# Layer 1's modulation products moved from the middle of a SwiGLU to its edges, in a two-layer diffusion block

## The chip, the cores and the metric

The kernel runs on one core of one Trainium2 chip. The metric is device time in microseconds (us) of one execution of the program. Every time below comes from the runs of the kernel before or from one profiled execution of it.

## The reference, cut to what matters

A block of two layers works on 512 latent tokens and 256 context tokens of width 1024. In each layer the stream is normalised, scaled and shifted by six modulation vectors that come from a conditioning vector `c` (for context tokens from `c_ctx`), goes through a mixer, and then the same again through a SwiGLU of width 2816. Layer 0's mixer is a long convolution beside a gating MLP. Layer 1's is a recurrent block, which puts out latent tokens only.

```python
def swiglu(h, w_in, w_out):
    z = h @ w_in
    return (jax.nn.silu(z[..., :D_FF]) * z[..., D_FF:]) @ w_out

silu_c = jax.nn.silu(c)
silu_cc = jax.nn.silu(c_ctx)
for l in range(DEPTH):
    mod_x = (silu_c @ w_ada[l] + b_ada[l]).reshape(-1, 1, N_MOD, D_MODEL)
    hx = modulate(rmsnorm(x, norm_mix_g[l]), mod_x[:, :, 0], mod_x[:, :, 1])
    ...
    x = x + mod_x[:, :, 2] * mix_x
    hx = modulate(rmsnorm(x, norm_ffn_g[l]), mod_x[:, :, 3], mod_x[:, :, 4])
    x = x + mod_x[:, :, 5] * swiglu(hx, w_ffn_in[l], w_ffn_out[l])
```

The change concerns `silu_c @ w_ada[l]` and `silu_cc @ w_ada[l]` for `l` = 1. `w_ada[1]` has 1024 x 6144 floats, 24 MB. Vectors 0 and 1 are needed when layer 1 begins, vector 2 when the recurrent block's result is added to the stream, vectors 3 to 5 in layer 1's SwiGLU.

## The kernel before, in words

Matrices are multiplied on PE in a split form: each operand becomes a high and a low part (`hh`/`hl`, `whi`/`wlo`), and three products (high by high, low by high, high by low) go into one accumulator. Weights come by DMA from SP's queue into `raw` tiles (lines 231 and 1420), and are split into `whi` and `wlo` by ACT, DVE and POOL (lines 248 and 249). PSUM has two `mm` tiles of two banks and four `sm` tiles of one bank (lines 208 to 212).

**Modulation products.** `Ada(l, r)` makes modulation vectors 2r and 2r+1 of layer l, for `c` and `c_ctx`, as one set, in eight steps k. `load(k)` brings a piece of `w_ada` of 128 x 2048 floats, 1 MB, from SP's queue (line 329). `mm(k)` makes four matmuls of 128 rows by 32 columns, each over 512 elements, side by side in one `sm` tile that is held until the eighth step (line 338; the trace has two records for each of these matmuls). After the eighth, ACT copies the tile to `adas` (line 342), PE transposes it in four pieces, and DVE adds `b_ada` into `mod[l][r]`. For layer 1 the loads go through one buffer of 8 KB a partition, of which `adas` is a use too, so a load waits for the matmuls of the step ahead of it.

**Where they stand before.** `fill` is a list of 24 steps, `Ada(1, 0)`, `Ada(1, 1)` and `Ada(1, 2)` in a row. `ffn` is layer 0's SwiGLU on 768 tokens. It takes 22 pairs of columns in parts of four (`PARTS`, line 59): for each pair the two input products and the gating, and after each part the part's share of the output product, with weights `wfo`. `post(j)` pops one step after pair j, or two.

**The order of the work.** Programs are written as Python loops, and a scheduler orders each engine's instructions by dependencies and by the priorities of the places that are written down. Each engine then runs its instructions in that order and waits where the next one isn't ready. SP issues all these DMAs in one order too.

**What surrounds the new places.** `Norm.start` (line 423) begins a layer half: it applies the norm to the first block of tokens for k = 0 to 7, with the first products of each k behind it, then to the second block; in the middle of the first loop it makes the second block's statistics (`stats`, matmuls with `ones`, line 394) and broadcasts them (`bc`, line 402, the transposes of `ny`). `out_units` (line 1079) is a generator over the tiles of an output projection, and `out_proj` runs all of it. In the recurrent stage `mix` interleaves the head products of chunk j+1 with a chain of units: input products, gate products, and output-projection units `w_out`. Between chunks, tiles change partitions by the DMAs `hx<-xl` and `th<-tg` on SP. The last units, `w_out(9, 11)`, come after the loop over 11 chunks.

## Time and profile before

| | |
|---|---|
| median of 3 runs | 1840.28 us (1839.06 to 1844.47) |
| profiled execution, own time | 1839.97 us |
| its span, first to last instruction | 1838.2 us |
| mean granted TensorE clock | 0.959 of full speed |
| PE busy | 1695.2 us, 92% of the span |
| DVE busy | 1271.3 us, 69% |
| ACT busy | 726.6 us, 40% |
| POOL busy | 622.0 us, 34% |
| DMA on SP's and the other hardware queues | 204.67 MB |

In the span, layer 0's SwiGLU begins at about 475 us; its pairs end at about 1028. The last of its output products lasts to about 1051, layer 1's norm and first products to 1087. The recurrent stage runs from there to about 1420, its last out-projection to 1433, and layer 1's SwiGLU and the final norm take the rest.

Busy time of an engine is the sum of its instructions, and of PE it overlaps, since matmuls are pipelined. "Idle before" in a timeline is the time that the engine waited ahead of the instruction, with what ended the wait. A granted clock of 1.00 is 2.4 GHz, 0.50 is 1.2 GHz; a stretch's figure is a mean of the two.

### The profile page before, as it was taken

To read this page: it belongs to the slowest core of one execution; us is meant where nothing else is said; L and a number is where in the kernel's file an instruction comes from. 1 tells how busy PE (TensorE), PEld (TensorE's weight loads), DVE (VectorE), ACT (ScalarE), POOL (GpSimd) and SP (SyncE) were. 2 spreads that over 40 slices of the span, in tenths; PEclk is the share of its full clock that TensorE was granted. 3 is DMA by queue.
4 is the path that set the end of the run, shared out by engine and by line. 5 is a ranking of instruction groups with operands and counts; after the bars stand their busy time and mean duration, and the time that the engine had idled before them with its cause. 6 is when DMAs were issued, how large, how long until landed. Compare 5 with 4: busy or idle time off the path is not lost. (4 is left out here: it accounts for less than half of the span.)

```text
span 1838.2 us, 23815 instructions
## 1 busy us (share of the span) xinstructions
PE 1695.2 (92%) x8968; PEld 1436.0 (78%) x8968; DVE 1271.3 (69%) x1963; ACT 726.6 (40%) x1144; POOL 622.0 (34%) x518
## 2 busy tenths in 40 slices
PE   5999999889989999999999897988986799999996
PEld 2576888679878989898899776777775778888885
DVE  7875766684887878887888876789888733333225
ACT  3543332222443333433343436665754332322212
POOL 4333132442455555564645412343353200000002
PEclk8999999999999999999999998988998899999998
DMA  8746232634223342224321224444443132222321
GB/s 288 232 139 233 89 120 72 245 111 150 78 106 115 116 147 105 69 92 132 143 71 63 74 80 116 121 124 121 113 119 104 47 122 96 92 92 81 91 81 46
DMA packets 78396, 213.00 MB, mean 116 GB/s; under 512 B 7609, under 2 KB 33353, under 8 KB 74185
## 3 DMA queue, kind: packets, MB, share of 16 engines
q1 hardware_dynamic: 75913, 204.67, 34.3%
q0 software_dynamic: 1792, 6.29, 1.0%
q8 instruction: 70, 1.15, 0.3%
q10 hardware_dynamic: 576, 0.52, 0.1%
q14 instruction: 45, 0.37, 0.1%
HBM read 178.30 MB, written 11.53 MB: 103 GB/s over the span
## 5 line engine op out<-in xcount | busy, mean ns | idle before, releaser
L249 DVE TENSOR_TENSOR wlo<-raw,whi 128x512 fp32r<-128x512 f32 (+2 forms) x300 | 310.0, 1050 | 264.3 <-ACT whi L248 257.0
L248 ACT CAST whi<-raw 128x1024 fp32r<-128x1024 f32 (+2 forms) x228 | 193.5, 858 | 430.4 <-PE mm L264 179.5
L387 POOL TENSOR_TENSOR ssum<-ssum,sq 128x256 f32<-128x256 f32 (+2 forms) x37 | 37.4, 1015 | 448.0 <-ACT sq L385 417.0
L249 POOL TENSOR_TENSOR wlo<-raw,whi 128x1024 fp32r<-128x1024 f32 (+1 forms) x31 | 77.7, 2506 | 129.4 <-DVE whi L248 42.6
L1110 PE MATMUL sm<-yh,whi 128*128 128x256 f32 (+1 forms) x304 | 97.5, 327 | 21.3 <-DVE x L1073 12.9
L287 PE MATMUL sm<-hh,whi 128*128 128x512 f32 (+1 forms) x248 | 94.9, 383 | 10.3 <-ACT whi L248 5.7
L1110 PE MATMUL sm<-yl,whi 128*128 128x256 f32 (+1 forms) x304 | 96.8, 318 | 2.5 <-DVE yl L257 2.5
L1110 PE MATMUL sm<-yh,wlo 128*128 128x256 f32 (+1 forms) x304 | 96.3, 317 | 0.0
L287 PE MATMUL sm<-hh,wlo 128*128 128x256 f32 (+1 forms) x248 | 92.8, 380 | 3.5 <-POOL wlo L249 2.8
L287 PE MATMUL sm<-hl,whi 128*128 128x512 f32 (+1 forms) x248 | 93.5, 377 | 0.0
L338 PE MATMUL sm<-ada,sct 128*32 128x512 f32 x384 | 77.6, 630 | 4.7 <-DMA ada<-in_w_ada_dram 3.0
L248 DVE CAST whi<-raw 128x512 fp32r<-128x512 f32 (+2 forms) x103 | 70.9, 688 | 15.9 <-PE sm L1285 12.1
L1110 PEld LDWEIGHTS sm<-yh,whi 128*128 128x128 f32 x304 | 60.9, 202 | 26.2 <-DVE x L1073 14.1
L264 PE MATMUL mm<-hl,whi 128*128 128x512 f32 (+1 forms) x256 | 69.4, 346 | 0.0
L264 PE MATMUL mm<-hh,wlo 128*128 128x512 f32 (+1 forms) x256 | 69.1, 347 | 0.0
L264 PE MATMUL mm<-hh,whi 128*128 128x512 f32 (+1 forms) x256 | 68.1, 345 | 0.0
L287 PEld LDWEIGHTS sm<-hh,whi 128*128 128x128 f32 x248 | 50.5, 203 | 21.0 <-ACT whi L248 8.1
L1651 ACT ACTIVATE tg<-mm,hba 88x768 f32<-88x768 f32 x64 | 55.3, 892 | 23.4 <-PE mm L264 13.3
L1110 PEld LDWEIGHTS sm<-yl,whi 128*128 128x128 f32 x304 | 61.7, 203 | 2.7 <-DVE yl L257 2.7
L1110 PEld LDWEIGHTS sm<-yh,wlo 128*128 128x128 f32 x304 | 61.4, 202 | 0.1
L287 PEld LDWEIGHTS sm<-hh,wlo 128*128 128x128 f32 x248 | 50.4, 204 | 12.6 <-POOL wlo L249 3.2
L1327 POOL TENSOR_TENSOR u<-u,u 128x384 f32<-128x384 f32 x40 | 51.4, 1285 | 25.5 <-ACT u L1326 25.5
(942 smaller groups left out, 5307.9 us busy)
## 6 DMA issues: line engine op xcount, KB each, us to landing
raw<-in_wfi_dram SPq DMA_DIRECT2D x88, 512.0 KB
ada<-in_w_ada_dram SPq DMA_DIRECT2D x32, 1024.0 KB
raw<-in_wfo_dram SPq DMA_DIRECT2D x38, 512.0 KB
ada<-in_w_ada_dram SPq DMA_DIRECT2D x24, 512.0 KB
raw<-in_wio_dram SPq DMA_DIRECT2D x22, 512.0 KB
raw<-in_wie_dram SPq DMA_DIRECT2D x20, 512.0 KB
th<-tg SPq DMA_DIRECT2D x12, 528.0 KB
kk<-kdx SPq DMA_DIRECT2D x16, 384.0 KB
```

Of the source, the lines that this page charges most:

```text
L248: (h_.tensor_copy if h_ is not act else act.copy)(hi, src)
L249: l_.tensor_sub(lo, src, f(hi))
L264: pe.matmul(o, w, xx, start=(k == 0 and pi == 0), stop=(k == n - 1 and pi == 2))
L287: pe.matmul(self.outs[b], w[:, k * P:(k + 1) * P], x, start=(n == 0 and pi == 0), stop=(n == self.nk - 1 and pi == 2))
L338: pe.matmul(self.ps[32 * q:32 * q + 32, :], sct[:, 2 * k:2 * k + 32], self.w[k, q], start=(k == 0), stop=(k == KD - 1))
L387: (dve if late else pool).tensor_add(self.s[b], self.s[b], q)
L1110: pe.matmul(pa, w[:, c], x[k][:, t0 - off:t1 - off], start=(i == 0 and pi == 0), stop=(i == n - 1 and pi == 2))
L1327: pool.tensor_add(v, v, u)
L1651: act.activation(h3(t[:, mi, :]), m[0:RDH, :, 0:384], AF.Tanh, bias=hba[:, b:b + 1], scale=0.5)
```

## The change

The steps no longer lie in a list that the SwiGLU's pairs pop. `Ada.units()` is a generator of eight units; each makes one step's products and then issues the next step's load. Set 0 is handed to `Norm.start` of layer 0's SwiGLU, which takes one unit at every second k of both loops. Set 1 (`late`) gives four units in layer 0's last output projection and four in layer 1's `Norm.start`. Set 2 (`last_mods`) goes in the recurrent loop, two units in chunk 8, two in chunk 9 and four in chunk 10. The buffer's pool `adaB` is opened later, in space that the convolution stage frees, and closed later. `g4`, which needs set 1, is computed after layer 1's start.

```diff
@@ -1,3 +1,4 @@
+import itertools
 import math
 
 import numpy as np
@@ -358,6 +359,15 @@
                 return go
             return [step(k) for k in range(KD)]
 
+        def units(self):
+
+            self.load(0)
+            for k in range(KD):
+                self.mm(k)
+                if k + 1 < KD:
+                    self.load(k + 1)
+                yield
+
     def ab(l, which):
         g = pc(f"mix_g{l}" if which == "mix" else f"ffn_g{l}")
         sc = mod[l][0][:, :, 8:16] if which == "mix" else mod[l][2][:, :, 0:8]
@@ -420,22 +430,26 @@
                 dve.scalar_tensor_tensor(hl[:, c], ta[:, c], self.sh[:, v, k:k + 1], f(hh[:, c]),
                                          op0=ALU.add, op1=ALU.subtract)
 
-        def start(self, jobs, order=range(KD), then=None):
+        def start(self, jobs, order=range(KD), then=None, fill=iter(())):
 
             for i, k in enumerate(order):
                 self.apply(0, k)
                 for j in jobs:
                     j.mm(0, k)
+                if i % 2:
+                    next(fill, None)
                 if i == 3:
                     self.stats(1)
                 if i == 6:
                     self.bc(1)
-            for k in order:
+            for i, k in enumerate(order):
                 self.apply(1, k)
                 if then:
                     then(k)
                 for j in jobs:
                     j.mm(1, k)
+                if i % 2:
+                    next(fill, None)
 
     def htiles(pl):
         hh = [pl.tile([P, T], F32R, tag=f"hh{k}", name=nm("hh")) for k in range(KD)]
@@ -1055,8 +1069,6 @@
     _, c2 = op("c2")
     _, xp = op("x")
     cm_xc, xc = op("xc")
-    cm_ada, ada["p"] = op("adaB")
-    ada.update(b=1, w=2048)
     cm_nt, ntp = op("ntB")
     cm_g, gp = op("g0")
     xt = []
@@ -1141,8 +1153,10 @@
     out_proj(lambda m: A["woe"][m], [4, 5, 6, 7, 0, 1, 2, 3], yh, yl, 0, mod[0][1][:, :, 0:8], FB0, nrm, 6)
     cl(cm_za)
     cl(cm_zb)
-
-    def ffn(l, blks, nrm, ntp, gp, hf, fill, done, nblks):
+    cm_ada, ada["p"] = op("adaB", "right")
+    ada.update(b=1, w=2048)
+
+    def ffn(l, blks, nrm, ntp, gp, hf, fill, late, done, nblks):
 
         off, h = blks[0][0], blks[0][1] - blks[0][0]
         n = 2 * h
@@ -1203,17 +1217,12 @@
         def halves(m):
             return [m[:, 0, n0], m[:, 1, n0]]
 
-        def post(j):
-            for left in (0, max(NPAIR - 2 - j, 0)):
-                if len(fill) > left:
-                    fill.pop(0)()
-
         wi, wo = A[f"wfi{l}"], A[f"wfo{l}"]
         W["eng"] = act, pool
         mA, mB = mmt(), mmt()
         o1 = [smt()[:, n0] for _ in range(2)]
         order = [k for r in range(KH) for k in (r, r + KH)]
-        nrm.start([job(wi[0], halves(mA)), job(wi[NPAIR], halves(mB)), job(wi[1], o1)], order, combine)
+        nrm.start([job(wi[0], halves(mA)), job(wi[NPAIR], halves(mB)), job(wi[1], o1)], order, combine, fill)
 
         def plain(j):
 
@@ -1396,7 +1405,6 @@
                     dve.tensor_sub(u, u, t12)
                     split(*g[2], t3)
                     split(*g[3], u)
-                post(j)
 
             W["eng"] = act, dve
             for j in range(p0, p1):
@@ -1405,10 +1413,15 @@
                 if j < 2 or last and j == p1 - 1:
                     flush()
             if last:
+                for _ in fill:
+                    pass
                 ntp = done()
                 nr = Norm(ntp, nblks, nb=(2, 4)[l])
-                out_proj(lambda m: wo[m, :, p0:p1, :], range(np_), [a for a, _ in gs], [b for _, b in gs], off,
-                         mod[l][2][:, :, 8:16], nblks, nr, most=(2, 4)[l])
+                for i, _ in enumerate(out_units(lambda m: wo[m, :, p0:p1, :], range(np_), [a for a, _ in gs],
+                                                [b for _, b in gs], off, mod[l][2][:, :, 8:16], nblks, nr,
+                                                most=(2, 4)[l])):
+                    if i % 4 == 3:
+                        next(late, None)
                 return nr
             W["eng"] = act, dve
             mg = mod[l][2][:, :, 8:16]
@@ -1533,7 +1546,7 @@
     dve.tensor_scalar_mul(cq2, ee, -4.0)
     dve.tensor_scalar_mul(hba, hba, 0.5)
     cl(cm_sp)
-    fill = Ada(1, 0).steps() + Ada(1, 1).steps() + Ada(1, 2).steps()
+    late = Ada(1, 1).units()
     cm_hf, hf = op("hf0")
 
 
@@ -1542,15 +1555,12 @@
         cm, p_ = op("ntC")
         return p_
 
-    nrm = ffn(0, FB0, nrm, ntp, gp, hf, fill, tail0, SEGC)
+    nrm = ffn(0, FB0, nrm, ntp, gp, hf, Ada(1, 0).units(), late, tail0, SEGC)
     cm_nn = opened[-1]
 
     cm_h, hp = op("h1", "right")
     hh, hl = htiles(hp)
     nrm.mods(1, "mix", xt, blocks(hh, hl, SEGC))
-
-    g4 = c2.tile([P, 2, 8], F32, name="g4")
-    dve.tensor_scalar_mul(g4, mod[1][1][:, :, 0:8], 0.25)
     rcw, rcb = pc("rcw"), pc("rcb")
     XL, HX, HW, TH = {}, {}, {}, {}
 
@@ -1614,8 +1624,12 @@
         mm_ = mmt()
         m = [mm_[:, 0, 0:LC], mm_[:, 1, :]]
         jobs.append((Job(A["wio"][NR + j], KD, blocks(hh, hl, SEGC), m), m))
-    nrm.start([j for j, _ in jobs])
-    for cm in (cm_nn, cm_g, cm_nt, cm_ada, cm_xc):
+    nrm.start([j for j, _ in jobs], fill=late)
+    for _ in late:
+        pass
+    g4 = c2.tile([P, 2, 8], F32, name="g4")
+    dve.tensor_scalar_mul(g4, mod[1][1][:, :, 0:8], 0.25)
+    for cm in (cm_nn, cm_g, cm_nt, cm_xc):
         cl(cm)
     _, wx = op("wx")
     W["raw"].append(wx)
@@ -1735,6 +1749,7 @@
         for g in gens:
             yield from g
 
+    last_mods = Ada(1, 2).units()
     mix(heads(0), chain(xl_units(2), pg_units(0), pg_units(1)), 20)
     for j in range(NR):
         a, b = rg_chunk(j)
@@ -1750,6 +1765,9 @@
         if j in (4, 7, 10):
             gens.append(w_out(j - 4, j - 1))
             n += 16
+        if j > 7:
+            gens.append(itertools.islice(last_mods, (2, 2, 4)[j - 8]))
+            n += (2, 2, 4)[j - 8]
         hs = heads(j + 1) if j + 1 < NR else []
         mix(hs, chain(*gens), n)
     W["slots"].append(wx)
@@ -1757,6 +1775,9 @@
     W["eng"] = act, dve
     cl(cm_rg)
     cl(cm_h)
+    for _ in last_mods:
+        pass
+    cl(cm_ada)
     cm_nt, ntp = op("ntD", "right")
     cm_g, gp = op("g1", "right")
     nrm = Norm(ntp, BLK1, nb=4)
```

The first place is PE's order at the begin of layer 0's SwiGLU, where the first block's products begin. `ny` and `ssum` belong to the norm's statistics, `b0h` to the first tokens' input, `sct` holds the conditioning vectors. The kernel after:

```order
L1122 MATMUL sm_4293<-yh_3707,wlo_4181 128x384
L412 MATMUL sm_4322<-ident,ny_4249 128x128 x3
L288 MATMUL mm_4431<-b0h_4394,whi_4437 128x384
L288 MATMUL mm_4432<-b0h_4394,whi_4443 128x384
L288 MATMUL sm_4433<-b0h_4394,whi_4449 128x384
L339 MATMUL sm_4487<-ada_4485,sct 32x512 x4
L404 MATMUL sm_4532<-ones,ssum_3882 128x1 x3
L288 MATMUL mm_4431<-b0l_4395,whi_4437 128x384
```

A set's first group (four matmuls) now stands ahead of the second block's statistics. In the kernel before no such group stood here.

The second place is PE's order some 220 rows on, at the end of the begin, first before and then after:

```order
L287 MATMUL sm_4434<-c3l_4417,whi_4449 128x384
L287 MATMUL sm_4434<-c3h_4416,wlo_4450 128x384
L338 MATMUL sm_4792<-ada_4883,sct 32x512 x4
L1285 MATMUL sm_4925<-b0h_4394,whi_4899 128x384
L1285 MATMUL sm_4925<-b0l_4395,whi_4899 128x384
L287 MATMUL mm_4805<-b0h_4394,whi_4808 128x384
L287 MATMUL mm_4805<-b0l_4395,whi_4808 128x384
```

```order
L1294 MATMUL mm_4961<-c3l_4417,whi_4948 128x384
L1294 MATMUL mm_4961<-c3h_4416,wlo_4949 128x384
L339 MATMUL sm_4487<-ada_4774,sct 32x512 x4
L346 MATMUL sm_4824<-ident,adas_4822 128x128 x4
L1294 MATMUL sm_4959<-b0h_4394,whi_4933 128x384
L1294 MATMUL sm_4959<-b0l_4395,whi_4933 128x384
L1294 MATMUL sm_4959<-b0h_4394,wlo_4934 128x384
```

Before, the third group of a set stood here and pair 2's products `sm<-b0h` followed at once. Now the eighth group and the four transposes of `adas` stand ahead of them. Between groups five and six, six and seven and seven and eight of the kernel after lie 37, 23 and 12 matmuls.

The third place is the end of the recurrent stage, PE's order in the kernel after. `yh_11498` to `yh_12092` are chunks 6 to 8, `yh_12219` on are chunks 9 and 10:

```order
L1122 MATMUL sm_12528<-yh_11672,wlo_12492 128x256
L1122 MATMUL sm_12528<-yh_12092,whi_12491 128x256
L1122 MATMUL sm_12528<-yl_12093,whi_12491 128x256
L1122 MATMUL sm_12528<-yh_12092,wlo_12492 128x256
L339 MATMUL sm_12179<-ada_12549,sct 32x512 x4
L339 MATMUL sm_12179<-ada_12555,sct 32x512 x4
L346 MATMUL sm_12563<-ident,adas_12561 128x128 x4
L1122 MATMUL sm_12586<-yh_12219,whi_12582 128x256
L1122 MATMUL sm_12586<-yl_12220,whi_12582 128x256
L1122 MATMUL sm_12586<-yh_12219,wlo_12583 128x256
```

The last two groups and the transposes now stand ahead of `w_out(9, 11)`, whose first rows are the last three; before, the units of chunks 6 to 8 were followed by these at once. Nine matmuls lie between the sixth group and the seventh, none between the seventh and the eighth.

On SP, in the same stretch of the kernel after:

```order
L1107 DMA raw_12580<-in_woo_dram 128x2x256
L330 DMA ada_12190<-in_w_ada_dram 128x2048
L1671 DMA th_12172<-tg_12148 40x1536
L330 DMA ada_12298<-in_w_ada_dram 128x2048
L1671 DMA th_12137<-tg_12227 88x1536
L1107 DMA raw_12607<-in_woo_dram 128x2x256
L1671 DMA th_12172<-tg_12267 88x1536
L1107 DMA raw_12635<-in_woo_dram 128x2x256
L330 DMA ada_12304<-in_w_ada_dram 128x2048
L1107 DMA raw_12663<-in_woo_dram 128x2x256
L232 DMA raw_12834<-in_wfi_dram 128x1024
L330 DMA ada_12543<-in_w_ada_dram 128x2048
```

Four of set 2's loads stand here among the weight loads and the transfers `th<-tg`; the last two follow further down, among the weight loads of layer 1's SwiGLU.

## Rows read from the trace of the kernel before

**Rows 1.** Windows of one part each: us; busy us (x instructions) by engine; PEclk; DMA share; GB/s.
```profile
540.40:638.60 98.20, 96.37 (x532) 87.85 (x531) 80.32 (x118) 37.27 (x72) 53.81 (x45) 0.98 0.34 116
638.60:740.50 101.90, 101.36 (x557) 87.95 (x556) 82.02 (x116) 39.17 (x75) 54.54 (x46) 1.00 0.37 126
740.50:837.30 96.80, 93.36 (x521) 88.40 (x520) 82.59 (x121) 38.85 (x75) 55.47 (x46) 1.00 0.26 86
837.30:939.20 101.90, 101.76 (x559) 88.37 (x558) 81.00 (x116) 39.13 (x75) 54.74 (x46) 1.00 0.37 126
```

**Rows 2.** The same windows, the products' line L338 alone: us, PE, PEld, PEclk, DMA share.
```profile
540.40:638.60 98.20, 6.17 (x32) 0.81 (x32) 0.98 0.34 116
638.60:740.50 101.90, 12.65 (x56) 1.76 (x56) 1.00 0.37 126
740.50:837.30 96.80, 1.07 (x8) 0.16 (x8) 1.00 0.26 86
```

**Rows 3.** Waits of PE from 740 to 840: us in total, times, longest.
```profile
PE sm L1285 <- ACT q1h L256: 1.2, 1, 1.2
```

**Rows 4.** Timeline of PE: start us, duration us, line, operation, count.
```profile
500.37 0.34 PE L287 MATMUL sm<-q0h,whi 128*128 128x384 f32 x1
500.64 1.06 PE L338 MATMUL sm<-ada,sct 128*32 128x512 f32 x8
...
501.91 0.34 PE L287 MATMUL mm<-q0h,wlo 128*128 128x384 f32 x1
...
639.90 0.34 PE L1285 MATMUL mm<-c3h,wlo 128*128 128x384 f32 x1
640.17 1.04 PE L338 MATMUL sm<-ada,sct 128*32 128x512 f32 x2
...
641.42 0.33 PE L1285 MATMUL sm<-t0l,whi 128*128 128x384 f32 x1
```

**Rows 5.** One 1 MB load: SP's timeline, SP's waits from 494, and a window.
```profile
494.28 0.33 SPq L329 DMA_DIRECT2D ada<-in_w_ada_dram  x1
...
SPq L329 <- DMA ada<-in_w_ada_dram: 4.5, 1, 4.5
...
495.20:498.80 3.60, 3.60 (x23) 3.60 (x21) 3.39 (x6) 2.56 (x5) 3.37 (x4) 1.00 0.84 291
```

**Rows 6.** Timeline of PE at the begin of layer 0's SwiGLU; idle before in brackets.
```profile
472.82 0.34 PE L1110 MATMUL sm<-yh,wlo 128*128 128x384 f32 x1
...
476.97 0.83 PE L394 MATMUL sm<-ones,ssum 128*128 128x1 f32 x6 [0.95 <-DVE ssum L387]
...
511.68 0.44 PE L1285 MATMUL sm<-b0h,whi 128*128 128x384 f32 x1 [2.78 <-DVE whi L248]
...
514.19 0.66 PE L1285 MATMUL sm<-b4h,whi 128*128 128x384 f32 x1 [1.55 <-DVE whi L248]
```

**Rows 7.** Window at the begin of layer 0's SwiGLU, columns as in group 1.
```profile
490.00:540.00 50.00, 42.00 (x229) 34.76 (x227) 46.67 (x54) 24.53 (x45) 32.72 (x25) 0.93 0.30 106
```

**Rows 8.** Window over the last out-projection of layer 0 and layer 1's begin.
```profile
1030.00:1090.00 60.00, 51.84 (x259) 43.04 (x258) 49.97 (x98) 23.73 (x41) 16.21 (x11) 0.89 0.22 69
```

**Rows 9.** Chain that ended last, recurrent stage: start us, us, what.
```profile
1384.22 4.11 DMA th<-tg
```

**Rows 10.** Timeline of PE at the end of the recurrent stage.
```profile
1416.02 0.39 PE L1110 MATMUL sm<-yh,whi 128*128 128x256 f32 x1 [1.05 <-DVE x L1073]
...
1420.64 1.22 PE L1110 MATMUL sm<-yh,whi 128*128 128x256 f32 x4 [4.00 <-ACT yh L256]
...
1421.88 0.41 PE L1110 MATMUL sm<-yh,wlo 128*128 128x256 f32 x1
1422.09 0.41 PE L1110 MATMUL sm<-yl,whi 128*128 128x256 f32 x1
...
1427.03 0.28 PE L1110 MATMUL sm<-yh,whi 128*128 128x256 f32 x1
1427.15 0.28 PE L1110 MATMUL sm<-yl,whi 128*128 128x256 f32 x1
```

## The prediction

> **What bounds the kernel now.** I read the time part by part first, then what ends PE's waits in each, then the timeline of single groups of products. The changed stretch is layer 0's SwiGLU, which goes in parts of four pairs. In four windows of one part's length each, cut near the same place of the cycle, PE is busy for 93.36 to 101.76 us of 96.80 to 101.90 [rows 1], and DVE for no more than 82.59: PE sets the pace there. The same windows, cut to the line of the modulation products [rows 2], show which parts carry them. The second window holds 56 records and 12.65 us of them, the third 8 records and 1.07 us (two records are one matmul). The third is the shorter, 96.80 against 101.90 us, but PE is idle in it for 96.80 - 93.36 = 3.4 us, in waits for ACT and DVE of which the longest is 1.2 us [rows 3]. So products fill, in the parts that have them, waits that come back in a part that has none. That is the main caution against costing them at their full busy time.
>
> A second reading is what one group of products costs on a busy PE [rows 4]. One matmul alone lies between matmuls that start at 639.90 and 641.42. Two ordinary matmuls of 0.173 us are in that stretch too, so the group costs 1.52 - 0.35 = 1.17 us. Four matmuls of a step, kept together, cost 501.91 - 500.37 - 0.35 = 1.19 us. A group costs the same whether it is whole or split, and the scheduler had split the eight steps of a set into up to 13 groups.
>
> A third is the load. Each step needs 1 MB through one buffer. Issued at 494.28, 0.33 us long, followed by a wait of 4.5 us for its landing: 4.85 us from issue to use, of which 3.6 us is transfer at 0.84 of the 16 engines [rows 5]. With one buffer, step k+1's load cannot be issued before step k's last matmul.
>
> **The change, part by part.**
>
> *Taken out of the SwiGLU.* From 540.4 on, the kernel before has 32 + 56 + 8 records in three windows, and in the fourth as many as in the second [rows 2]. The third part without its 1.07 us group and its transposes would take about 95.5 us; this is my yardstick for a part with none. The first part gives 98.20 - 95.5 = 2.7, the second 6.4, the third 1.3, the fourth 6.4 [rows 1]: **-17 us**. Bounds: if PE's waits grow so that a part goes no lower than the 96.80 that was seen, 1.4 + 5.1 + 5.1 = 11.6; if no wait takes the products' place, all their busy time, 6.17 + 12.65 + 1.07 + 12.65 = 32.5 [rows 2]. The third part still had one of the four `sm` accumulators lent to a set of products, which the changed kernel doesn't lend there, so the upper end is not excluded. I take the yardstick, as it is the nearest row. The loads taken off SP here cost nothing: PE hardly waited for weights.
>
> *Set 0 at the begin.* Its eight groups now stand between the first products of the stretch and those of pair 2; before, five of them lay ahead of 540. The first load must wait for the last matmul of the out-projection (it reads a tile in the freed space): 472.82 + 0.34 [rows 6], plus 4.85, lands at 478.0. The two weight loads queued behind it on SP are for products after 511. PE stands in order at this group, and the statistics behind it, at 476.97 before [rows 6], go at 479.2: +2.2. The second group adds 1.2 ahead of the transposes that release the second block's normalisation. Groups 2 to 4 stand where three groups stood. Groups 5 to 7 add 3 x 1.19 = 3.6. Group 6 follows group 5 after 23 matmuls (4.0 us) and group 7 follows after 12 (2.1 us), with 4.85 us of load in each gap: 0.9 + 2.8 of waiting. The copy and four transposes before pair 2's 24 matmuls are 2 by estimate. In all 3.4 + 3.6 + 3.7 + 2 = 12.7. Against it stand PE's waits for DVE's weights, 2.78 and 1.55 [rows 6], and the low clock: a mean of 0.93 over 50 us [rows 7] is 7 us at 1.2 GHz, half of which, 3.5, comes back if PE is fed there. 12.7 - 4.3 - 3.5 = **+5**. DVE is busy for 46.67 of 50 [rows 7], so a late normalisation is not made up soon; but what is late on PE alone hides behind DVE. Bounds 0 and +10.
>
> *Set 1 in the out-projection and at layer 1's begin.* Eight groups, 9.5; waits for loads where few matmuls lie between groups (3.2 us of them ahead of group 5, 2.3 ahead of group 7, against 4.85): 1.6 + 2.5; copy and transposes 2. PE's idle time in this stretch is 60 - 51.84 = 8.2 [rows 8], and several groups stand right ahead of such a wait. 9.5 + 4.1 + 2 - 8.2 = 7.4; I take **+6**, since feeding PE lifts the clock of 0.89 [rows 8] a little. SP's order puts set 2's first load, which waits for the copy of set 1, ahead of the five transfers `hx<-xl` that start the recurrent stage; that is inside the same lateness. Bounds +2 (idle takes nearly all) and +9.
>
> *Set 2 at the end of the recurrent stage.* Groups 0 to 4 fall into waits that PE has there for DVE. By the order, group 4 stands near 1406, group 5 can follow at 1406 + 1.1 + 4.85 = 1412, group 6 at 1418, inside the idle 4.00 us ahead of 1420.64 [rows 10], group 7 at 1424. With copy and transposes, 2, the last out-projection `w_out(9, 11)` starts at 1427 in place of 1420.64: **+6.5**. What is queued behind it on PE is all that is left of the stage, and DVE's normalisation of layer 1's SwiGLU waits for that. Bounds: +2 if group 4 runs some 4.5 us earlier, +10 if it runs 3.5 us later.
>
> *DMA.* As many bytes as before, but three of set 2's loads now stand on SP among `th<-tg` transfers, one of which is on the chain that ended last, 4.11 us [rows 9]; a transfer that finds a 1 MB load ahead of it is late by up to 3.6 us [rows 5]. I cost that at nothing, as the loads are issued one per chunk and the chain has one such transfer in a chunk; it is in the rival below. The multiplication for `g4` moves to a place with slack.
>
> Sum: -17 + 5 + 6 + 6.5 = +0.5. The profiled execution took 1839.97 us, 0.3 under the median of 1840.28, so both give **1840.5 us**.
>
> The DMA length is where the Trainium skill, page "DMA: Bandwidth & Descriptors", section "Measured (HBM→SBUF, 128 partitions, SWDGE, issued from GpSimd)", would have it otherwise. It lists 6.15 us for 1 MB. As an estimate from that page, the eight exposed loads above (three, two, three) would each be 1.3 us longer and the sum +11, 1851 us. The page's figure is for another issuing path, and the trace's 4.85 stands here.
>
> **The rivals.**
> *Faster (0.31).* The SwiGLU gives back 22 to 25 rather than 17, as no accumulator is lent and the waits of the third part are its own, and the begin hides behind DVE: -22 + 2 + 4.5 + 4 = -11.5, **1828.5**. For it: DVE has 14 us of slack in a part [rows 1], and one group of waits is only 1.2 long [rows 3]. Against it: the third part ran without products and did wait 3.4.
>
> *Slower (0.22).* The one-buffer chain at the end of the recurrent stage. It decides from group 4: each microsecond that it comes after 1406 moves group 7 and `w_out(9, 11)` by as much, since three loads of 4.85 and three groups follow one after the other. If one `th<-tg` ahead of its load on SP holds it for 4 us, and a load in turn holds a transfer of the chain for 3.6, the end is at +0.5 + 4 + 3.6 = +8, **1848.5**. For it: SP issues in order. Against it: DVE, not PE, leads this stage up to 1420, so there is room.
>
> *The clock (0.07).* In `w_out(9, 11)` matmuls start 0.21 us apart at first and 0.12 apart later [rows 10]: 1.2 and 2.4 GHz, the former after 4.00 us of idling. If sparse products with waits for loads hold the low level for its first 70 matmuls more, that is 70 x 0.09 = +6.5, and **1847**. The Trainium skill has such a rule, "TensorE: Matmul & The Clock Gate", section "HAM oscillation — how this bites in real kernels": matmuls in short bursts with waits for DMA between them keep falling back to the low clock, and it speaks against this change.
>
> **How the numbers follow.** About 0.3%, 5.5 us, is what a measurement of this kernel can tell from no change. My forecast's case, edges that give back what the SwiGLU gains, within that bound: 0.36. The faster rival is 0.31, the two slower ones 0.29, and 0.04 is left to mishaps that I have not seen, half to each side: faster 0.33, same 0.36, slower 0.31. All bounds together would give -32.5 + 0 + 2 + 2 = -28.5 and -11.6 + 10 + 9 + 10 = +17.4; they won't all fall on one side, so I give 1824 to 1853. The forecast's own range is 1835 to 1846.
>
> **What would show it.** In the profile after: parts of the SwiGLU of about 95 to 96 us each with PE's waits for ACT and DVE at the start of the out-products; less than 94 is the faster rival, 97 or more the slower bound. At the begin, a wait of 2 us for `ada` ahead of the statistics and one of some 3 us ahead of the eighth group; the second block's transposes 3.4 us later after the out-projection's end than before. At the end of the recurrent stage, groups 5, 6 and 7 some 6 us apart, each with a wait for the load, and `w_out(9, 11)` behind them. It is wrong if these groups are all done before `yh` is ready (then the time is 1834 or less), if a `th<-tg` takes over 6 us, or if the parts don't shrink.

## The result and the profile after

The changed kernel takes 1851.34 us, the median of 7 runs (1848.94 to 1862.11), beside 1839.61 for the kernel before in the same session: a ratio of 1.008, with a 95% interval of 1.006 to 1.010. Run again beside the experiments it gave 1.006 (1.0041 to 1.0080). So it is slower by some 11 to 15 us. 1840.5 and no change had been forecast; the time lies in the range, near its upper end, and a loss is shown where none was forecast.

The page of the profiled execution, parts 1 and 4, shows first where not to look. PE has less to do than before (1695.2 us there): the products' groups are no longer split, and layer 1's sets take 29.4 us of PE in place of 37.9. The span is longer all the same, and a row that was not there before stands in the chain of waits: DMA of `ada`.

```profile
span 1849.6 us, 23807 instructions
...
PE 1689.9 (91%) x8968; PEld 1435.5 (78%) x8968; DVE 1273.6 (69%) x1963; ACT 725.6 (39%) x1144; POOL 629.5 (34%) x518
...
PE mm L265 13%; PE sm L1501 6%; PE sm L1122 2%; DMA ada<-in_w_ada_dram 1%; PE sm L288 1%; PE mm L288 1%; DVE whi L249 0%; PE sm L339 0%; DMA th<-tg 0%; DVE th L1690 0%; DVE th L1710 0%; DVE xl L1579 0%; DVE th L1691 0%; DVE T L1703 0%; DVE xlo L258 0%
```

To place the loss, six instructions that both programs have are enough. The timelines of the kernel before show five of them (start us, duration us, engine, line, operation, idle before); the sixth, the first matmul of `w_out(9, 11)`, is the second row of [rows 10].

```profile
475.23 0.61 PE L287 MATMUL mm<-b0h,whi 128*128 128x384 f32 x2 [1.41 <-ACT b0h L418]
...
538.41 0.54 DVE L1320 TENSOR_TENSOR s<-s,sm 128x384 f32<-128x384 f32 x1
...
1052.38 0.68 PE L402 MATMUL sm<-ident,ny 128*128 128x128 f32 x4 [1.46 <-DVE ny L305]
...
1090.07 0.83 ACT L256 CAST xh<-hx 88x768 fp32r<-88x768 f32 x1 [7.48 <-DMA hx<-xl]
...
1419.97 0.62 ACT L256 CAST yh<-th 128x512 fp32r<-128x512 f32 x1 [7.23 <-DVE th L1701]
```

The same in the kernel after, with the sixth:

```profile
477.22 0.61 PE L288 MATMUL mm<-b0h,whi 128*128 128x384 f32 x2 [1.42 <-ACT b0h L428]
...
549.63 0.55 DVE L1329 TENSOR_TENSOR s<-s,sm 128x384 f32<-128x384 f32 x1 [1.14 <-PE sm L1294]
...
1046.14 0.71 PE L412 MATMUL sm<-ident,ny 128*128 128x128 f32 x4 [3.05 <-DVE ny L306]
...
1091.68 0.83 ACT L257 CAST xh<-hx 88x768 fp32r<-88x768 f32 x1 [8.89 <-DMA hx<-xl]
...
1420.66 0.62 ACT L257 CAST yh<-th 128x512 fp32r<-128x512 f32 x1 [3.41 <-DVE th L1715]
...
1430.77 0.56 PE L1122 MATMUL sm<-yh,whi 128*128 128x256 f32 x1
```

They are the first product of layer 0's SwiGLU, DVE's first evacuation of pair 2 (DVE takes a finished product out of PSUM), the broadcast of layer 1's first norm, the first head's cast behind `hx<-xl`, the last cast to `yh`, and the first matmul of `w_out(9, 11)`. The table has the time from each to the next. (Before the first of them PE's order is the same in ten of the kernels of this document, yet its time lies between 471.3 and 477.2 in their profiles. In whole_before, six_tail_back and six_dense, which also reorder layer 0's products, it is 480.0, 483.3 and 484.7. So profiles are compared from there on.)

| us | begin | SwiGLU and its last out-projection | layer 1's begin | recurrent stage | `yh` to `w_out(9, 11)` |
|---|---|---|---|---|---|
| before | 63.2 | 514.0 | 37.7 | 329.9 | 0.7 |
| after | 72.4 | 496.5 | 45.5 | 329.0 | 10.1 |
| difference | +9.2 | -17.5 | +7.9 | -0.9 | +9.4 |

The middle of the SwiGLU gives 17.5 us, and the three places to which the products went take 9.2, 7.9 and 9.4. The rest of the 11.4 us between the spans is 2.0 ahead of the first of the six instructions and 1.2 behind the last.

**The middle.** Windows of the kernel after, one part each (columns as in [rows 1]):

```profile
627.90:724.50 96.60, 92.72 (x506) 89.11 (x505) 84.41 (x117) 38.20 (x74) 55.27 (x46) 0.98 0.22 66
724.50:821.20 96.70, 92.58 (x506) 88.99 (x505) 84.84 (x117) 38.18 (x74) 55.80 (x46) 0.98 0.21 66
```

A part takes 96.6 to 96.7 us, and PE is idle for 4 of them. Two of the windows of [rows 1] together, 638.6 to 837.3, took 198.7 and held a set's 13 groups; two now take 193.3. So a set gives back 5.4 of the 13 x 1.18 = 15.3 us that its groups took on PE. More than for a set comes from the first part. Its end, the ninth `s<-s,sm` of DVE, before and then after:

```profile
641.48 0.54 DVE L1320 TENSOR_TENSOR s<-s,sm 128x384 f32<-128x384 f32 x1
...
647.08 0.54 DVE L1329 TENSOR_TENSOR s<-s,sm 128x384 f32<-128x384 f32 x1
```

From pair 2's first evacuation to there it is 103.1 us before and 97.4 after, 5.6 less. The stage also holds three of set 1's groups, in the last out-projection. They cost nothing there: from PE's first wait for `u` in it (1029.33 before, 1023.73 after) to the broadcast it is 23.1 us before and 22.4 after. The pairs alone give 16.8.

**The begin.** PE's timeline, and DVE's row behind it:

```profile
478.62 1.07 PE L339 MATMUL sm<-ada,sct 128*32 128x512 f32 x8 [0.61 <-DMA ada<-in_w_ada_dram]
...
542.85 1.06 PE L339 MATMUL sm<-ada,sct 128*32 128x512 f32 x8 [0.23 <-DMA ada<-in_w_ada_dram]
544.62 0.66 PE L346 MATMUL sm<-ident,adas 128*128 128x128 f32 x4 [0.71 <-ACT adas L343]
545.03 0.42 PE L1294 MATMUL sm<-b0h,whi 128*128 128x384 f32 x1
...
545.32 0.25 DVE L349 TENSOR_TENSOR mod<-sm,prm 128x16 f32<-128x16 f32 x2 [3.46 <-PE sm L346]
```

PE's waits for `ada` are short, 0.61 and 0.23. But pair 2's first product, which stood at 511.68 before [rows 6], stands at 545.03, behind the transposes, and DVE waits 3.46 for them. Nor do the groups fill PE's waits. The stage as a window before, after and in begin_six, an experiment below (columns as in [rows 1]):

```profile
475.20:538.40 63.20, 54.14 (x295) 46.17 (x296) 58.16 (x93) 28.59 (x56) 35.49 (x27) 0.95 0.27 92
477.20:549.60 72.40, 59.51 (x322) 47.95 (x323) 59.91 (x100) 29.61 (x57) 37.45 (x27) 0.91 0.43 147
472.70:535.20 62.50, 57.32 (x317) 47.49 (x318) 57.77 (x92) 28.76 (x56) 36.24 (x27) 0.95 0.41 145
```

PE is idle for 9.1 us before and for 12.9 after, and the granted clock falls from 0.95 to 0.91.

**Layer 1's begin.** ACT and SP in the kernel before, then ACT, SP and DVE in the kernel after, where the heads' input goes out:

```profile
1080.24 2.35 ACT L1564 ACTIVATE xl<-mm,prm 128x256 f32<-128x256 f32 x4
1085.86 8.18 SPq L1575 DMA_DIRECT2D hx<-xl  x4
...
1078.55 2.35 ACT L1574 ACTIVATE xl<-mm,prm 128x256 f32<-128x256 f32 x4
...
1084.35 0.33 SPq L330 DMA_DIRECT2D ada<-in_w_ada_dram  x1
1085.33 0.93 SPq L1585 DMA_DIRECT2D hx<-xl  x1
...
1084.00 0.26 DVE L349 TENSOR_TENSOR mod<-sm,prm 128x16 f32<-128x16 f32 x2 [0.97 <-PE sm L346]
...
1085.22 0.17 DVE L1631 TENSOR_SCALAR g<-mod 128x16 f32<-128x16 f32 x1
```

The first evacuation of `xl`, on ACT, is 4.5 us later than before, counted from the broadcast. From it to the first `hx<-xl` it is 6.8 us in place of 5.6, as DVE makes `mod` and `g` in between. From there to the cast it is 1091.68 - 1085.33 = 6.3 in place of 4.2: SP had issued a 1 MB load 1 us ahead.

**The end of the recurrent stage.** The chain of waits (start us, us, what):

```profile
1407.37 6.96 DMA ada<-in_w_ada_dram
...
1415.50 4.84 DMA ada<-in_w_ada_dram
...
1422.38 4.94 DMA ada<-in_w_ada_dram
```

and PE's timeline there:

```profile
1414.38 1.06 PE L339 MATMUL sm<-ada,sct 128*32 128x512 f32 x8 [1.53 <-DMA ada<-in_w_ada_dram]
...
1420.38 1.93 PE L339 MATMUL sm<-ada,sct 128*32 128x512 f32 x8 [3.67 <-DMA ada<-in_w_ada_dram]
1427.36 1.94 PE L339 MATMUL sm<-ada,sct 128*32 128x512 f32 x8 [5.04 <-DMA ada<-in_w_ada_dram]
1430.00 1.11 PE L346 MATMUL sm<-ident,adas 128*128 128x128 f32 x4 [0.71 <-ACT adas L343]
```

`yh` is ready at 1421.3, but PE's order has two groups ahead of what needs it. Three loads stand in a row on the chain, 6.96, 4.84 and 4.94 us. PE does one group between them, and behind the first of these groups nine short matmuls of chunks 6 to 8. After idling 3.67 and 5.04 us the groups take 1.93 and 1.94 us, not 1.06; the granted clock is 0.50 in both, and 1.00 in the group at 1414.38.

### The profile page after: what moved, and what is told of

Its sections match the earlier page's. It is cut to its first block, busy times and chain, and to the rows that moved or that the text cites. A ratio compares the mean times of both kernels' runs of the same rounds, so it can differ in the third digit from the quotient of the medians.

```text
span 1849.6 us, 23807 instructions
## 1 busy us (share of the span) xinstructions
PE 1689.9 (91%) x8968; PEld 1435.5 (78%) x8968; DVE 1273.6 (69%) x1963; ACT 725.6 (39%) x1144; POOL 629.5 (34%) x518
## 5 line engine op out<-in xcount | busy, mean ns | idle before, releaser
L250 POOL TENSOR_TENSOR wlo<-raw,whi 128x1024 fp32r<-128x1024 f32 (+1 forms) x31 | 79.5, 2565 | 122.0 <-DVE whi L249 44.8
L288 PE MATMUL sm<-hh,whi 128*128 128x256 f32 (+1 forms) x248 | 94.8, 383 | 5.1 <-ACT whi L249 4.0
L1122 PE MATMUL sm<-yh,wlo 128*128 128x256 f32 (+1 forms) x304 | 95.5, 315 | 0.0
L288 PE MATMUL sm<-hl,whi 128*128 128x256 f32 (+1 forms) x248 | 93.9, 379 | 0.0
L339 PE MATMUL sm<-ada,sct 128*32 128x512 f32 x384 | 70.2, 673 | 18.9 <-DMA ada<-in_w_ada_dram 17.5
```

Of the source, the lines that this page charges most:

```text
L250: l_.tensor_sub(lo, src, f(hi))
L288: pe.matmul(self.outs[b], w[:, k * P:(k + 1) * P], x, start=(n == 0 and pi == 0), stop=(n == self.nk - 1 and pi == 2))
L339: pe.matmul(self.ps[32 * q:32 * q + 32, :], sct[:, 2 * k:2 * k + 32], self.w[k, q], start=(k == 0), stop=(k == KD - 1))
L1122: pe.matmul(pa, w[:, c], x[k][:, t0 - off:t1 - off], start=(i == 0 and pi == 0), stop=(i == n - 1 and pi == 2))
```

## The experiments

My theory: at the end of the recurrent stage it is the one-buffer chain of loads, at the begin the late normalisation and the groups, at layer 1's begin the groups and the load ahead of `hx<-xl`. The rivals were that loads and groups cost the same wherever they stand, and that lateness at an edge is made good later. Each experiment gives its stages as in the table above.

| us | begin | SwiGLU | layer 1's begin | recurrent | wait of `w_out(9, 11)` | ratio to before (95%) |
|---|---|---|---|---|---|---|
| before | 63.2 | 514.0 | 37.7 | 329.9 | 0.7 | 1 |
| after_again | 72.4 | 497.1 | 45.0 | 329.5 | 10.7 | 1.006 (1.0041 to 1.0080) |
| tail_early | 73.2 | 496.5 | 44.8 | 341.6 | 0.7 | 1.0084 (1.0062 to 1.0105) |
| early_small | 72.7 | 496.6 | 45.0 | 332.9 | 0.7 | 1.005 (1.0031 to 1.0069) |
| tail_noload | 72.4 | 496.2 | 45.3 | 330.4 | 0.7 | 1.001 (0.9994 to 1.0027) |
| tail_back | 73.8 | 499.4 | 44.5 | 327.4 | 0.7 | 1.0009 (0.9997 to 1.0021) |
| begin_back | 64.3 | 504.7 | 44.6 | 328.0 | 9.1 | 1.0032 (1.0016 to 1.0049) |
| begin_six | 62.5 | 498.2 | 40.6 | 328.4 | 13.7 | 1.0015 (1.0004 to 1.0027) |
| late_back | 81.8 | 500.3 | 38.4 | 326.4 | 10.2 | 1.0069 (1.0054 to 1.0084) |
| six_tail_back | 63.0 | 496.4 | 44.2 | 325.8 | 0.7 | 0.9984 (0.9973 to 0.9996) |
| whole_before | 62.7 | 505.8 | 37.9 | 324.7 | 0.7 | 0.9976 (0.9962 to 0.9989) |
| six_dense | 63.1 | 503.8 | 37.8 | 324.5 | 0.7 | 0.9953 (0.9936 to 0.9970) |

The stages have a spread of their own. Five of these kernels have no modulation products in the recurrent stage (before, tail_back, six_tail_back, whole_before, six_dense), and they take 324.5 to 329.9 there. So less than some 5 us in that column tells nothing by itself.

**after_again**: no edit.

> The changed kernel again, unchanged, beside the next three on the same chip. If its 0.8% is the change and not the first chip, 1.006 to 1.010 of the kernel before.

The loss is the change's.

**tail_noload**, the first on the end of the recurrent stage, leaves out the last three loads of set 2 (its last steps then use step 4's weights):

```diff
-        def units(self):
+        def units(self, top=KD):
...
+                for q in range(4):
+                    self.w[k, q] = self.w[min(k, top - 1), q]
                 self.mm(k)
-                if k + 1 < KD:
+                if k + 1 < top:
-    last_mods = Ada(1, 2).units()
+    last_mods = Ada(1, 2).units(5)
```

> The changed kernel, but steps 5 to 7 of set 2 use step 4's piece of w_ada and make no load, so three loads of 1 MB are left out and vector 2r of set 2 is wrong. Theory (the loads' time is what PE waits for): groups 5 to 7 follow at once, PE's waits of 1.5, 3.7 and 5.0 us for ada vanish, w_out(9, 11) starts by 1422, 9 us less than the changed kernel, 1842. Rival (it is the groups at the low clock, the copy and the transposes in PE's order): at most 3 us less, 1848.

The wait is gone, and with it most of the loss: 1.001 in place of 1.006 to 1.008. PE's timeline shows the last four steps' groups in a row but for two records, and `w_out(9, 11)` waits for `yh` alone:

```profile
1401.88 4.52 PE L339 MATMUL sm<-ada,sct 128*32 128x512 f32 x30
...
1412.98 0.60 PE L346 MATMUL sm<-ident,adas 128*128 128x128 f32 x4
...
1417.67 1.23 PE L1124 MATMUL sm<-yh,whi 128*128 128x256 f32 x4 [1.93 <-ACT yh L257]
```

So it is the loads' time. Groups, copy and transposes fit in. A second buffer for the loads was not tried.

**tail_early**, the same set placed where no later work waits for it:

```diff
-        if j > 7:
-            gens.append(itertools.islice(last_mods, (2, 2, 4)[j - 8]))
-            n += (2, 2, 4)[j - 8]
+        if 4 < j < 9:
+            gens.append(itertools.islice(last_mods, 2))
+            n += 2
```

> The changed kernel with set 2 two steps earlier per chunk, two units each in chunks 5 to 8 in place of 2, 2 and 4 in chunks 8 to 10. Theory (the one-buffer chain of loads ahead of w_out(9, 11) is what costs the end of the recurrent stage, 1430.77 - 1420.64 = 10.1 us, of which 0.7 is older): w_out(9, 11) starts when yh is ready, about 9.4 us less than the changed kernel's 1851.3, 1842, and no wait of PE for ada of over 1 us after 1390. Rival (1 MB loads on SP hold th and hx transfers wherever they stand, or the groups cost PE time in this stage): the stage up to chunk 8 grows by what the end loses, 1848 to 1852.

A miss: `w_out(9, 11)` starts with `yh`, as the theory said, but the recurrent stage is 12.6 us longer than in the changed kernel, and nothing is won. The waits of all engines in the last third of that stage name the transfers between partitions. In tail_early (us in total, times, longest):

```profile
ACT T L1688 <- DMA th<-tg: 23.4, 6, 8.2
```

and in the kernel before:

```profile
ACT T L1674 <- DMA th<-tg: 14.0, 6, 3.6
```

**early_small** is tail_early with a quarter of each load of set 2, the rest left out. It tells the transfer from the order on SP:

```diff
+            if self.l == 1 and self.r == 2:
+                w = ada["p"].tile([P, 2048], F32, tag="ada", bufs=ada["b"], name=nm("ada"))
+                nc.sync.dma_start(w[:, 0:512], A["w_ada"][1, P * k:P * (k + 1), 4096:4608])
+                for q in range(4):
+                    self.w[k, q] = w[:, 0:512]
+                return
```

> tail_early (set 2 in chunks 5 to 8), but each of set 2's eight loads brings only the first 512 of 2048 columns, 0.25 MB, and the four matmuls of a step use it four times; the rest of w_ada's third is left out, so set 2 is wrong. Order and waits on SP stay. Theory (in tail_early the 1 MB loads delay th transfers on the DMA engines: ACT waited 23.4 us for th there, longest 8.2, against 14.0 and 3.6 before): the recurrent stage loses its 9 to 11 us, 8 us less than tail_early, about 1844. Rival (SP, which issues in order, holds the transfers behind the loads' waits, or PE's groups and the held sm tile cost): at most 3 us less, 1850.

A quarter of the bytes, in the same places, gives back 8.7 of the 12.6 us of the stage. So most of it goes with the bytes of the loads and not with their place on SP. What makes the other 3.9 is open: the longest wait for `th` is 7.1 still, and 3.9 is within the stage's own spread.

**begin_back** undoes the begin:

```diff
+        def post(j):
+            for left in (0, max(NPAIR - 2 - j, 0)):
+                if len(steps) > left:
+                    steps.pop(0)()
...
+                post(j)
...
+    steps = Ada(1, 0).steps()
...
-    nrm = ffn(0, FB0, nrm, ntp, gp, hf, Ada(1, 0).units(), late, tail0, SEGC)
+    nrm = ffn(0, FB0, nrm, ntp, gp, hf, iter(()), late, tail0, SEGC)
```

> The changed kernel with set 0 back in the SwiGLU, one step per pair from pair 2 on; sets 1 and 2 stay where the change puts them. Theory (the begin loses some 8 us up to 540, from +2.0 to +10.2 on DVE, and the SwiGLU gives back about 5 for a set): 3 to 4 us less than the changed kernel, 1848, with DVE at 540 no later than in the kernel before and PE's parts 5 us longer in all. Rival (the begin's lateness is slack that the SwiGLU would have waited out anyway): 4 to 6 us more, 1856.

The begin is 8.1 shorter and the SwiGLU 8.2 longer. By the stages the move of set 0 wins nothing and loses nothing; by the ratios, 1.0032 against 1.006 and 1.008, it loses 5 to 9 us. That is more than the 3 to 4 us of the theory, and the rival, 4 to 6 us in the other direction, is out. The profiles don't show where it lies: 5 to 6 us of the difference stand ahead of the first of the six instructions, where PE's order is the same and the spread is as large.

**begin_six** leaves six of set 0's units where the change put them:

```diff
-        nrm.start([...], order, combine, fill)
+        nrm.start([...], order, combine, itertools.islice(fill, 6))
...
+        def post(j):
+            if j > 3:
+                next(fill, None)
```

> The changed kernel with six units of set 0 at the begin and the last two behind pairs 4 and 5, so that the transposes no longer take an sm tile ahead of pair 2, whose first products stand behind the fifth group again. Theory (at the begin it is this order that costs, not the loads, whose waits sum to 1.0 us; PE had no products for the waits up to 540 and DVE then waited 3.5 us for the transposes): DVE at 540 is 3 us late against the begin of the stretch and not 8.2, and the time is 3 to 5 us less than the changed kernel's. Rival (the lateness is from the first groups and the late normalisation): no less than 1 us below it.

The whole 9.2 us of the begin are gone, though the first group still waits for its load and stands ahead of the statistics. So the late normalisation cost nothing. The groups cost nothing either: the scheduler put the seventh group ahead of DVE's first evacuation of pair 2 too (at 535.21 here), so seven of the eight are still in the begin. They fill waits, as PE is idle for 5.2 us in the window above, and the clock is 0.95. What the edit took out of the begin is the eighth group, the copy and the transposes, 2.2 us of PE's time in the kernel after (542.85 to 545.03). The other 7 us come with the order. PE's first product of pair 2 is back among the first block's:

```profile
505.77 1.06 PE L339 MATMUL sm<-ada,sct 128*32 128x512 f32 x8
509.61 0.69 PE L1298 MATMUL sm<-b0h,whi 128*128 128x384 f32 x1 [2.77 <-DVE whi L249]
...
530.19 1.06 PE L339 MATMUL sm<-ada,sct 128*32 128x512 f32 x8
```

That the transposes' tile makes the order is read from the code and not shown by a run: two of the four `sm` tiles hold pair 1's products there and one holds set 0's; the transposes take the fourth, and pair 2 has to wait until they are done with. The end of the recurrent stage costs more here, 13.7: counted from the broadcast, `yh` comes 5.6 us earlier than in the changed kernel and the end of the chain of loads only 2.0.

**late_back** and **tail_back** are on layer 1's begin. The first sends set 1 back as begin_back does set 0 (`steps = Ada(1, 1).steps()`, `late = iter(())`), the second set 2 (one unit per pair from pair 6 on).

> The changed kernel with set 1 back in the SwiGLU, one step per pair from pair 2 on; sets 0 and 2 stay where the change puts them. Theory (the last out-projection and layer 1's begin lose some 8 us, from -5.3 to +2.6 on DVE, against about 5 that the SwiGLU gains): 3 us less than the changed kernel, 1848. Rival (the recurrent stage, which has slack, makes the lateness good, so only the SwiGLU's gain is lost): 5 us more, 1856.

> The changed kernel with set 2 alone back in the SwiGLU, one step per pair from pair 6 on. Theory (set 2 costs the end of the recurrent stage some 10 us, and its first load, on SP ahead of the hx<-xl transfers, most of what layer 1's begin loses): w_out(9, 11) starts when yh is ready; from the end of the SwiGLU to the first heads the kernel loses 2 to 3 us and not 8; the SwiGLU gives back 5 less. Some 10 us less than the changed kernel, 1838 to 1840, as the kernel before. Rival (layer 1's begin is late by set 1's own groups and loads): it loses the same 8 us there, and the time is 1843 to 1845.

Without set 1 layer 1's begin takes 38.4 in place of 45.5, so 7.1 of its 7.9 us come with set 1. late_back is no measure of the time, since its steps followed set 0's at once and the begin went to 81.8. In tail_back no load stands ahead of `hx<-xl`, and the cast follows after 4.3 us, not 6.3. The time is the theory's, 1839.9. Yet the stage keeps 44.5, as the rival has it: the load ahead of the transfers is not what makes it long.

Nor are set 1's groups the most of it. begin_six has all eight in the same stretch as the changed kernel, and the stage takes 40.6 there. Its ACT, DVE and SP:

```profile
1063.83 2.35 ACT L1580 ACTIVATE xl<-mm,prm 128x256 f32<-128x256 f32 x4
...
1065.10 6.88 DVE L1585 SCALAR_TENSOR_TENSOR xl<-mm,prm,xl 128x254 f32<-128x254 f32 x12
...
1073.07 0.25 DVE L349 TENSOR_TENSOR mod<-sm,prm 128x16 f32<-128x16 f32 x2 [1.10 <-PE sm L346]
...
1069.43 2.08 SPq L1591 DMA_DIRECT2D hx<-xl  x2
...
1073.10 0.35 SPq L330 DMA_DIRECT2D ada<-in_w_ada_dram  x1
```

Here DVE makes `mod` behind all twelve evacuations, not between them, and SP issues set 2's load behind the first two `hx<-xl`. Counted from the broadcast (1033.36) the first evacuation is 2.6 us later than before, not 4.5. From it to the first `hx<-xl` it is 5.6 us and from there to the cast 4.5, in place of 6.8 and 6.3. So 5 of the 7.9 us come with the order at set 1's end, which the scheduler gives, and some 2.9 with the eight groups and their loads. No run puts DVE's adds alone behind the evacuations.

**Towards a better kernel.** whole_before changes the kernel before in one place of the code, which layer 0's products pass through too:

```diff
-            for q in range(4):
-                pe.matmul(self.ps[32 * q:32 * q + 32, :], sct[:, 2 * k:2 * k + 32], self.w[k, q],
-                          start=(k == 0), stop=(k == KD - 1))
+            with tc.high_priority(offset=2000):
+                for q in range(4):
+                    pe.matmul(self.ps[32 * q:32 * q + 32, :], sct[:, 2 * k:2 * k + 32], self.w[k, q],
+                              start=(k == 0), stop=(k == KD - 1))
```

> The kernel before with one edit: the four matmuls of a step are put at a higher priority, so that each step stays one group, 24 groups for the three sets in place of 35; loads and places stay in the SwiGLU. Theory (a group costs 1.17 to 1.19 us of PE whether split or not, and the SwiGLU gives back somewhat under half of what is taken from PE there): 11 groups fewer are 13 us of PE, 4 to 7 us less than the kernel before, ratio 0.996 to 0.998. Rival (products that fill PE's waits are free, and whole groups fill them worse): no change or up to 3 us more.

It is 0.24% faster than the kernel before, and PE's time in the products of both layers falls from 77.6 us (the L338 row of the page's part 5) to 66.7 (groups by line: busy us, mean ns of one, idle before):

```profile
L339 PE MATMUL sm<-ada,sct 128*32 128x512 f32 x384 | 66.7, 620 | 4.6 <-DMA ada<-in_w_ada_dram 3.4 <-issue 1.3
```

All of that is layer 1's: its sets go from 37.9 us to 25.6, and layer 0's from 39.7 to 41.1. By the stages the SwiGLU gains 8.2 us. The recurrent stage gains 5.2 without an edit there, within its spread, and the stretch ahead of the first of the six instructions, where layer 0's products stand, loses 4.7.

six_tail_back and six_dense put begin_six's begin and whole groups together. Both have whole_before's priority; the first sends set 2 into the SwiGLU from pair 6 on, the second sets 1 and 2 (its edit is shown):

```diff
+            if j > 3:
+                next(fill if j < 6 else steps, None)
...
-    late = Ada(1, 1).units()
+    late = iter(())
+    steps = (u for r in (1, 2) for u in Ada(1, r).units())
```

> begin_six with set 2 in the SwiGLU from pair 6 on, a step's four matmuls at a higher priority so that they stay one group. Of the change there remain set 0's first six units at the begin and set 1. Theory (begin_six has left only the end of the recurrent stage, some 14 us on DVE, and the SwiGLU costs 4 to 5 for a set of whole groups): 9 us less than begin_six, 1830, ratio to the kernel before 0.994 to 0.997, as whole_before or a little under it. Rival (the end of the recurrent stage is bound by other transfers and only seems to be set by these loads): no more than 3 us less, 1836.

> six_tail_back with set 1 in the SwiGLU too: set 0's first six units at the begin and two behind pairs 4 and 5, sets 1 and 2 behind pairs 6 to 21, whole groups, each load issued a pair ahead; nothing of the change is left in the last out-projection, layer 1's begin or the recurrent stage. Theory (set 1's groups, its adds on DVE and its loads cost layer 1's begin 6 to 8 us, the SwiGLU 4 to 5 for a set of whole groups): 2 to 4 us less than six_tail_back, 1832, as whole_before. Rival (the last pairs have no room, so groups at the end of the SwiGLU push the output products): no less than six_tail_back's 1835.

six_tail_back goes from begin_six's 1.0015 to 0.9984, some 6 us where 9 had been expected and the stages add up to 13.3 less (930.1 against 943.4). The first of the six instructions comes 10.6 us later than in begin_six (483.3 against 472.7). The priority reorders layer 0's products ahead of it, in 36 groups and not 33, and in all three kernels with the priority it comes later than in any other. So the edit meant for layer 1 seems to lose several us in layer 0. No run has it in layer 1 alone. six_dense has the lowest time of all, 1828.6 us, 0.47% under the kernel before and some 1.1 to 1.3% under the changed one. Its interval and whole_before's overlap by a little, so what it adds to whole groups is not clear. What it keeps of the change is the prefetch (a load is issued right behind the products of the step ahead, a pair early) and the early start of set 0.

## Why the prediction was wrong

- **The SwiGLU's gain, -17.** Measured -17.5. The total held, in part by luck. A part without products took 96.7 and not 95.5, with PE idle for 4 us in it, which is my lower bound and not the yardstick: the second and third window gave 5.4 where I had 6.4 + 1.3. The first part made up for it with 5.6 where I had 2.7; why is open. The caution that waits come back in place of products was right: the full 32.5 was not to be had.
- **Set 0 at the begin, +5.** Measured +9.2, and by another mechanism. The terms "3.4" for the late statistics and "3.7" for waiting on loads were nothing: begin_six keeps the first, and the waits for loads are 0.61 and 0.23. The copy and transposes, "2 by estimate", are the step that failed. Behind them stood pair 2's products, and DVE in turn waits for the transposes. The order of the kernel after shows it; I priced what was added and not what was pushed back. With that the two credits failed as well: PE's waits were to take 4.3 and the clock to give back 3.5, but PE's idle time rose from 9.1 to 12.9 us and the clock fell from 0.95 to 0.91. In begin_six, with the order mended, the idle time falls to 5.2.
- **Set 1, +6.** Measured +7.9 at layer 1's begin and -0.6 in the out-projection. The number is near, the mechanism was not: I added up groups, waits for loads, copy and transposes and took off PE's idle time, but begin_six has the same groups and loses 2.9. I put DVE's adds at nothing by not naming them, and the load ahead of `hx<-xl` at "inside the same lateness"; in the profile they are 1.2 and 2.1 us. Without the load alone, in tail_back, the stage is hardly shorter (44.5).
- **Set 2 at the end, +6.5.** Measured +9.4, with the mechanism shown by tail_noload. Group 4 stood at 1406.24, as I had put it. The term that was mis-sized is the step from group to group: 8.1, 6.0 and 7.0 us in place of 5.9, because the first load took 6.96 us, not 4.85, among weight loads issued at 1406.82 and 1411.01, and because the last two groups ran at the low clock, granted 0.50, and took 1.93 in place of 1.06 us. The latter is what the Trainium skill's page "TensorE: Matmul & The Clock Gate", section "HAM oscillation — how this bites in real kernels", describes: bursts of matmuls with waits for DMA between them fall back to the low clock. The trace agrees here, at 0.9 us a group; that `w_out(9, 11)` would then stay slow did not come: its matmuls are 0.21 us apart for 2 us and 0.12 after that, as before.
- **The sum.** -17 was right to half a microsecond and the three costs were each too small, by 4.2, 1.9 and 2.9. The sum came out at +0.5 where the stages give +8.1. The Trainium skill's page "DMA: Bandwidth & Descriptors", section "Measured (HBM→SBUF, 128 partitions, SWDGE, issued from GpSimd)", with its 6.15 us for 1 MB (of the transfer alone, which took 3.6 here) would have made it +11 by my estimate, close to what was measured, but for a reason that the trace does not bear out: of eight loads that I had called exposed, PE waited 0.8 us in all for those at the begin.
- **The rivals.** The slower one had the right place and the wrong condition: group 4 was not late and no `th<-tg` on the chain was held. tail_early shows that the second half of it, a transfer behind a 1 MB load, is real where the loads stand earlier in the stage. The clock rival's sum is 6.3 and not 6.5 (70 x 0.09); it did not come either way.

## What to carry to other kernels

Before work is moved into idle time, look at what the moved work's last step holds (an accumulator, a tile, an engine's place in its order) and at what then stands behind it: the time is lost there, not in the work. A chain of loads through one buffer needs one step's full load time plus what shares the queues, here 6 to 8 us a step, ahead of anything that waits for its end. And where small products interrupt a dense stream of matmuls, count the interruptions: 24 in place of 35 gave 8.2 us in the SwiGLU with the products left in their place, and the time fell, where moving the products away made it rise. An edit of a shared function should be looked at wherever it is called: this one also changed layer 0.

## What the runs showed of the hardware

A group of products with 32 columns cost PE 1.17 to 1.19 us between matmuls, with one matmul in it or four. A 1 MB load took 4.85 us from issue to use when alone and 6.96 among other weight loads. A group of products took 1.06 us at a granted clock of 1.00 and 1.93 at 0.50, after PE had idled for 3.67 and 5.04 us. The recurrent stage, which waits for transfers between partitions, took 8.7 us longer with eight loads of 1 MB than with eight of 0.25 MB. And the time up to the same instruction, some 475 us in, differed by up to 6 us between profiled executions of ten kernels with one order on PE up to there, about half of what the change makes.
